# A hybrid encoder step on one core: 28 instead of 16 steps of the gates' projection ahead of the first attention scores, and two tiles instead of one for the near bias tables

## The chip, the core and the metric

The kernel runs on one core of a Trainium2 chip. A core has a matrix engine (TensorE, PE in the profile, its weight loads PEld), VectorE (DVE), ScalarE (ACT), GpSimd (POOL) and SyncE (SP). In this kernel SP and ACT issue nearly all DMA transfers. Each engine, and each issuing queue, works through its own list of instructions in order, and waits at an instruction until what that needs is there. The metric is the time of one execution in device microseconds (us), the median of several.

## The reference

One layer of an encoder over 2048 prompt rows and 32 sample rows, all in float32 (D_MODEL = 1024, 8 attention heads of 64 channels, chunks of 64 rows, each seeing itself and the 8 chunks before it). Cut to what matters here:

```python
h = rmsnorm(x, g_pre_mix) * (1 + scale_m) + shift_m
qa, ka, va, qb, kb, vb, gb, gk_low, gate_a, gate_b = split(h @ w_in)
bias = rel_bias[:, clip(i - j, -128, 128) + 128]                  # per head
ya = softmax(qa @ ka.T * 64 ** -0.5 + bias, over own + 8 chunks) @ va
yb = gated_linear_attention(qb, kb, vb, gk_low) ...
merged = sigmoid(gate_a) * (ya @ w_br_a) + sigmoid(gate_b) * (yb @ w_br_b)
x = x + gate_m * rmsnorm(merged @ w_out, g_post_mix)
x = x + gate_f * rmsnorm(conv_ffn(...), g_post_ffn)
```

## The kernel before

The activations `h` are kept on chip as a high and a low part (`hA`, `hB`, two arrays each); every product of matrices is three matmuls (`mm3`, L78 to L80): high x high, low x high, high x low. The program goes through five stages: the normalised input and a first projection, a projection with rows as outputs (`n_tile`, tiles `pn`), gated linear attention, band attention, and then merge, output projection and the gated MLP. PE's list is in the order in which the program is written; a scheduler orders the lists of the other engines and queues when the kernel is built.

**The near bias tables.** `bias_tables` (L454 to L473) is a generator, stepped once in every other `n_tile` through `side` beside `mod_late`, which streams rows of `w_ada` (tiles `wa2`, shown as `wa`) and adds them up on DVE (L484, L486). For each pair of heads `bias_tables` loads a tile `tr` from `rel_rev` (L464, issued by SP), turns it over with one matmul into `pb` (L467, two records each in the trace), writes `pb - cf` back into the same `tr` (L469, DVE), fills a corner (L471, DVE) and stores `tr` to `nbD` in DRAM (L472, issued by ACT). There is one buffer `tr`, so the load of a pair waits until the store of the pair before has landed.

**Attention and its filler.** `unit(h, g)` is one head's attention for 256 query rows (g = 8 is the sample); there are 72 units. A unit loads its queries (`q`, L977), every other unit a chunk of keys and values (L888, L892), and the first unit of a head the bias table `nb` (L908), all issued by SP. `scores` makes the scores of 128 query rows: matmuls into `PN` and `F` (L928, L929), bias and maximum on DVE (L936 to L944), the exponentials on ACT (L945, L948), the scaling of the tile `P` on POOL (L952). Each `P` is then transposed by PE (`pp`, L1019), split into two parts on ACT and DVE (`pth`, `ptl`) and multiplied with the values (`py`). Since the softmax of a unit takes a while, PE is given a filler between: `dense` with 16 chunks of 128 columns of the gates' projection (640 steps), then `branch_b` (160 steps). A step is one `mm3` of 128 x 416 outputs; eight steps make one output tile `pm`, which ACT passes through a tanh (L222) and stores to `sgT` (L230). A chunk is five tiles, so 40 steps; the weights of the next chunk are loaded (`wr`, L185) and split (L186 on ACT, L187 on DVE) while one runs.

The first unit has no unit before it, so its head is written out by hand (L1165 to L1172): the loads, 16 filler steps, the scores of its first 128 rows, 4 steps, its second scores, the loads of the next unit, 8 steps. What is left of the filler, `left`, is dealt out over the 72 units: a unit's quota follows from its own PE work, and within a unit its quota, its own transposes and products, the scores of the next unit (`S0_AT`, `S1_AT`) and the loads of the one after (`L_AT`) are sorted by due time.

Of the kernel before, what the change touches and what calls it, by code (L numbers as in the profile page):

```python
# [10 lines left out]
F32 = mybir.dt.float32  # L11
# [28 lines left out]
def dap(ap, offset, dims):  # L40
    return bass.AP(tensor=ap.tensor, offset=ap.offset + offset, ap=dims)
# [17 lines left out]
def encoder_step(ctx: ExitStack, tc: tile.TileContext, I, O):  # L59
    nc = tc.nc  # L60

    def pool(st, name, bufs=1, **kw):
        return st.enter_context(tc.tile_pool(name=name, bufs=bufs, reuse_waits="tile", **kw))
# [174 lines left out]
    with ExitStack() as st:  # L238
# [204 lines left out]
        wa = pool(late_st, "wada")  # L443
# [10 lines left out]
        def bias_tables():  # L454

            flip = wa.tile([128, 128], F32, name="flip")
            nc.gpsimd.memset(flip, 1.0)
            nc.gpsimd.affine_select(flip, flip, pattern=[[1, 128]], base=-127, channel_multiplier=1,
                                    compare_op=OP.is_equal, fill=0.0)
            cf = wa.tile([128, HA], F32, name="cf")  # L460
            nc.sync.dma_start(cf, dap(I["rel_rev"], 0, [[0, 128], [384, HA]]))
            for h in range(0, HA, 2):
                tr = wa.tile([128, 2, 256], F32, name="tr", tag="tr")
                nc.sync.dma_start(tr, dap(I["rel_rev"], h * 384, [[1, 128], [384, 2], [1, 256]]))  # L464
                yield
                p = psx.tile([128, 512], F32, name="pb", tag="px")
                nc.tensor.matmul(p, flip, tr.rearrange("p a b -> p (a b)"), start=True, stop=True)  # L467
                for j in range(2):
                    nc.vector.tensor_scalar(tr[:, j], p[:, 256 * j:256 * j + 256], cf[:, h + j:h + j + 1], None,  # L469
                                            op0=OP.subtract)  # L470
                nc.vector.memset(tr[0:64, :, 192:256], NEG)  # L471
                nc.scalar.dma_start(dap(nbD, h * 128 * 256, [[256, 128], [128 * 256, 2], [1, 256]]), tr)  # L472
                yield  # L473
# [76 lines left out]
        def side():  # L550

            yield from bias_tables()
            for blk in range(4, 12):
                yield from mod_late(blk)
            yield
            yield from mod_turn()
# [38 lines left out]
    def pull(stream, n):  # L595
        for _ in range(n):
            next(stream, None)
# [253 lines left out]
    with ExitStack() as st:  # L851
# [300 lines left out]
        def fill():  # L1152
            yield from dense(stg, [("g", i, 3088 + 128 * i) for i in range(16)], late_w.pop(1), ahead)
            yield from branch_b()

        filler = fill()
        units = [(h, g) for h in range(HA) for g in range(9)]
        left = 800 - 8
        us = [unit(*u) for u in units] + [None, None]

        def ustep(u):
            if u is not None:
                next(u)

        ustep(us[0])  # L1165
        pull(filler, 16)
        ustep(us[0])
        pull(filler, 4)
        ustep(us[0])
        ustep(us[1])  # L1170
        pull(filler, 8)
        left -= 28  # L1172

        own = [3 * {0: 3, 1: 6, 8: 3}.get(g, 9) for h, g in units]
        whole = (3 * left + sum(own)) / len(units)
# [1020 lines left out]
```

## Time and profile before

| | us |
|---|---|
| median of 3 executions | 3203.68 |
| lowest, highest | 3203.21, 3213.49 |
| the profiled execution, its own time | 3200.21 |
| span of its trace (first to last instruction) | 3198.5 |
| PE busy | 3075.2 |
| DVE busy | 2248.1 |
| ACT busy | 1654.4 |
| POOL busy | 550.0 |

The profile is one execution, taken by the hardware profiler. All instants below are us from the start of its span. PE's ends are modelled, so that a busy share of PE does not say that it runs at its peak. [...] A row of a timeline has the start, the duration, the engine, the line, the operation, what it writes and reads, and in brackets how long its engine was idle before it and what ended that.

### The profile page before, as it was taken

How to read it: one execution, taken by the hardware profiler on the slowest of the kernel's cores; microseconds unless marked ns; L12 is line 12 of the kernel's file. 1: busy time of each engine (PE TensorE's matmuls, PEld its weight loads, DVE VectorE, ACT ScalarE, POOL GpSimd, SP SyncE). 2: the span in 40 equal slices, each digit the busy share in tenths (PEclk: the TensorE clock that was granted, in tenths of full speed). 3: DMA queues.
4: the chain of work that ended last, by engine and by line, in shares of the span. 5: the costliest groups of instructions: out<-in, count | busy, mean ns of one | idle time of the engine just before them, and what ended most of it. 6: DMA issues, size and time to landing. Idle time of an engine off the chain costs nothing. (4 is left out here: it accounts for less than half of the span.)

```text
span 3198.5 us, 57346 instructions
## 1 busy us (share of the span) xinstructions
PE 3075.2 (96%) x19748; PEld 2963.9 (93%) x19748; DVE 2248.1 (70%) x4913; ACT 1654.4 (52%) x3856; POOL 550.0 (17%) x663
## 2 busy tenths in 40 slices
PE   6999999999999999999999899999999999999997
PEld 4899999998999999988999899999999999999997
DVE  6735517774555445566676799899888778998877
ACT  4412224443555545544444555567656556676755
POOL 2201201111111111111344433400000001310001
PEclk9999999999999999999999999999999999999998
DMA  7344435545333333576466676777987667888785
GB/s 224 104 137 129 141 104 137 140 127 139 110 114 102 101 97 114 163 230 197 131 191 190 207 246 208 227 240 223 263 246 217 192 189 207 273 248 287 236 276 148
DMA packets 601367, 580.21 MB, mean 181 GB/s; under 512 B 55761, under 2 KB 529570, under 8 KB 601074
## 3 DMA queue, kind: packets, MB, share of 16 engines
q1 hardware_dynamic: 556386, 528.93, 55.7%
q10 hardware_dynamic: 44432, 47.34, 4.6%
q8 instruction: 155, 2.54, 0.3%
q14 instruction: 138, 1.13, 0.1%
q0 software_dynamic: 256, 0.26, 0.0%
HBM read 388.71 MB, written 187.65 MB: 180 GB/s over the span
## 5 line engine op out<-in xcount | busy, mean ns | idle before, releaser
L78 PE MATMUL pm<-hA,wh 128*128 128x416 f32 x768 | 290.3, 378 | 0.0
L1740 PE MATMUL ad<-hA,hB 128*128 128x350 f32 (+2 forms) x1566 | 271.3, 324 | 6.7 <-ACT work L1866 3.4
L79 PE MATMUL pm<-hA,wh 128*128 128x416 f32 x768 | 270.2, 352 | 0.0
L80 PE MATMUL pm<-hA,wl 128*128 128x416 f32 x768 | 270.0, 352 | 0.0
L1682 DVE TENSOR_TENSOR hA<-raws,hA 128x512 fp32r<-128x512 f32 (+1 forms) x368 | 257.5, 708 | 16.5 <-ACT hA L1677 15.9
L1740 PEld LDWEIGHTS ad<-hA,hB 128*128 128x128 f32 x1566 | 255.2, 190 | 7.8 <-ACT work L1866 4.3
L1677 ACT ACTIVATE hA<-raws 128x512 fp32r<-128x512 f32 (+1 forms) x368 | 223.6, 617 | 36.0 <-DVE raws L1658 13.6
L1740 PE MATMUL ad<-hA,hA 128*128 128x348 f32 (+2 forms) x1362 | 235.0, 325 | 5.5 <-ACT g L1849 4.8
L1658 POOL TENSOR_TENSOR raws<-raws 128x512 f32<-128x512 f32 (+1 forms) x90 | 144.6, 1619 | 538.9 <-DMA raws<-in_w_down_dram 316.5
L1740 PE MATMUL g<-hA,hB 128*128 128x350 f32 (+2 forms) x1350 | 233.8, 323 | 3.0 <-ACT work L1862 1.6
L1740 PEld LDWEIGHTS ad<-hA,hA 128*128 128x128 f32 x1362 | 222.3, 190 | 7.0 <-ACT g L1849 5.1
L1740 PEld LDWEIGHTS g<-hA,hB 128*128 128x128 f32 x1350 | 218.8, 188 | 5.1 <-ACT work L1862 2.8
L1740 PE MATMUL ad<-hA 128*128 128x350 f32 (+2 forms) x1263 | 218.3, 323 | 4.4 <-ACT work L1866 4.3
L1740 PEld LDWEIGHTS ad<-hA 128*128 128x128 f32 x1263 | 204.5, 188 | 6.2 <-ACT work L1866 6.1
L1682 DVE TENSOR_TENSOR hB<-raws,hB 128x512 fp32r<-128x512 f32 (+1 forms) x287 | 203.5, 716 | 4.0 <-ACT hB L1677 3.9
L952 POOL TENSOR_SCALAR P<-P,mx 128x640 f32<-128x640 f32 (+5 forms) x136 | 103.3, 759 | 534.9 <-DVE mx L951 289.5
L1677 ACT ACTIVATE hB<-raws 128x512 fp32r<-128x512 f32 (+1 forms) x287 | 174.7, 616 | 27.3 <-DMA raws<-in_w_up_dram 11.0
L78 PE MATMUL pn<-wh,hA 128*128 128x256 f32 (+1 forms) x624 | 177.6, 285 | 0.0
L79 PE MATMUL pn<-wl,hA 128*128 128x256 f32 (+1 forms) x624 | 176.6, 283 | 0.0
L80 PE MATMUL pn<-wh,hA 128*128 128x256 f32 (+1 forms) x624 | 176.4, 283 | 0.0
L69 ACT ACTIVATE pth<-pp 128x256 fp32r<-128x256 f32 (+1 forms) x288 | 106.0, 373 | 133.6 <-PE pp L1019 123.1
L1849 ACT COPY g<-ad 128x348 f32<-128x348 f32 (+2 forms) x102 | 44.4, 435 | 230.7 <-PE ad L1740 154.2
(484 smaller groups left out, 8769.3 us busy)
## 6 DMA issues: line engine op xcount, KB each, us to landing
raws<-in_w_up_dram SPq DMA_DIRECT2D x220, 256.0 KB, 4.1
raws<-sW SPq DMA_DIRECT2D x176, 256.0 KB, 3.8
sW<-raws SPq DMA_DIRECT2D x88, 256.0 KB, 4.2
raws<-in_w_down_dram SPq DMA_DIRECT2D x80, 256.0 KB, 4.9
wr<-in_w_in_dram SPq DMA_DIRECT2D x76, 256.0 KB, 3.2
sgT<-tx ACTq DMA_DIRECT2D x80, 208.0 KB, 2.6
wa<-in_w_ada_dram SPq DMA_DIRECT2D x64, 256.0 KB, 2.9
keys<-ks SPq DMA_DIRECT2D x128, 128.0 KB, 3.0
```

The source lines that it names most:

```text
L69: i = nc.scalar.activation(hi, src, AF.Copy)
L78: nc.tensor.matmul(out, ah, bh, start=first and i == 0, stop=False)
L79: nc.tensor.matmul(out, ah, bl, start=False, stop=False)
L80: nc.tensor.matmul(out, al, bh, start=False, stop=last and i == n - 1)
L952: nc.gpsimd.tensor_scalar(P[:m, :tot], P[:m, :tot], mx[:m, 6:7], 1.0, op0=OP.mult, op1=OP.mult)
L1658: getattr(eng, op)(raw(out, n), raw(a, n), raw(b, n))
L1677: act = nc.scalar.activation(hi[:, :n], raw(i, n), AF.Copy)
L1682: nc.vector.tensor_sub(lo[:, :n], raw(i, n), f32(hi[:, :n]))
L1740: nc.tensor.matmul(out[:, :w], l_[:, k], r_[:, k, :w], start=first and k == 0 and i == 0, stop=k == n - 1 and i == 2, skip_group_check=True)
L1849: nc.scalar.copy(g[:, 0, :w], ad[:, 0, :w])
```

## The change

The diff, whole:

```diff
@@ -460,7 +460,7 @@
             for h in range(0, HA, 2):
-                tr = wa.tile([128, 2, 256], F32, name="tr", tag="tr")
+                tr = wa.tile([128, 2, 256], F32, name="tr", tag="tr", bufs=2)
                 nc.sync.dma_start(tr, dap(I["rel_rev"], h * 384, [[1, 128], [384, 2], [1, 256]]))
@@ -1163,13 +1163,13 @@
         ustep(us[0])
-        pull(filler, 16)
+        pull(filler, 28)
         ustep(us[0])
         pull(filler, 4)
         ustep(us[0])
         ustep(us[1])
         pull(filler, 8)
-        left -= 28
+        left -= 40
```

`tr` gets a second buffer, so that the load of a pair of heads waits for the store two pairs before. In the head of attention 28 steps of the filler stand between the loads of the first unit and its first scores. No operation is added or taken away. The 12 steps come out of the units' quotas: the units with g = 2 and g = 6 of each head (16 units) have 8 steps instead of 9, and the units (1,0), (3,0), (5,0) and (7,0) 15 instead of 14; the other 52 keep their number.

On SP's queue, at the first loads of the bias tables (`cf`, `tr`, then the stream of `wa` and the weights `wr` of the next projection), the difference is:

```order
 L461 DMA cf<-in_rel_rev_dram 128x8x1
-L464 DMA tr<-in_rel_rev_dram 128x2x256
+L464 DMA tr<-in_rel_rev_dram 128x2x256 x2
 L481 DMA wa_2000<-in_w_ada_dram 128x512
 L481 DMA wa_2004<-in_w_ada_dram 128x512
 L481 DMA wa_2059<-in_w_ada_dram 128x512
+L185 DMA wr<-in_w_in_dram 128x2x256 x2
 L481 DMA wa_2063<-in_w_ada_dram 128x512
```

The second table is loaded right behind the first; the third and the fourth load stand where the second and the third stood (behind `wa_2402` and `wa_2662`), and the place of the fourth is empty. Two weight loads go ahead of a `wa`.

On ACT, at the head of attention (`tx` is the tanh of a filler tile and `sgT` its store, `vs` the split of values, `P` the exponentials, `pth` the split of a transposed `P`, `wh` the split of the next chunk's weights), before:

```order
L222 ACTIVATE tx<-pm 128x416
L230 DMA sgT<-tx 128x416
L900 ACTIVATE vs<-vr 128x4x64
L945 ACTIVATE P,mx<-P,mx 128x128
L945 ACTIVATE P,mx<-P,mx 128x256
L900 ACTIVATE vs<-vr 128x4x64
L222 ACTIVATE tx<-pm 128x416
L230 DMA sgT<-tx 128x416
L69 ACTIVATE pth<-pp 128x256
```

and in the changed kernel, from the same place on:

```order
L222 ACTIVATE tx<-pm 128x416
L230 DMA sgT<-tx 128x416
L945 ACTIVATE P,mx<-P,mx 128x128
L900 ACTIVATE vs<-vr 128x4x64
L222 ACTIVATE tx<-pm 128x416
L230 DMA sgT<-tx 128x416
L945 ACTIVATE P,mx<-P,mx 128x256
L900 ACTIVATE vs<-vr 128x4x64
L186 ACTIVATE wh<-wr 128x512
L222 ACTIVATE tx<-pm 128x416
L186 ACTIVATE wh<-wr 128x512
L69 ACTIVATE pth<-pp 128x256
```

Here a `tx` with its store stands ahead of each of the first two exponentials, and the split of the weights of the chunk after next (`wh`, twice) stands ahead of the first `pth` instead of behind the exponentials of the next unit.

On SP, at the head of attention, before:

```order
L892 DMA vr<-vn 128x4x128
L977 DMA q_8757<-qs 128x256
L977 DMA q_8859<-qs 128x256
L977 DMA q_8965<-qs 128x256
L888 DMA keys_8746<-ks 64x512 x2
L888 DMA keys_8747<-ks 64x512 x2
L892 DMA vr<-vn 128x4x128
L977 DMA q_9099<-qs 128x256
L888 DMA keys_8746<-ks 64x512 x2
L888 DMA keys_8747<-ks 64x512 x2
```

and in the changed kernel:

```order
L977 DMA q_8757<-qs 128x256
L977 DMA q_8902<-qs 128x256
L977 DMA q_9019<-qs 128x256
L888 DMA keys_8746<-ks 64x512 x2
L888 DMA keys_8747<-ks 64x512 x2
L892 DMA vr<-vn 128x4x128
L888 DMA keys_8746<-ks 64x512 x2
L888 DMA keys_8747<-ks 64x512 x2
L977 DMA q_9139<-qs 128x256
```

Up to the queries of the first unit (`q_8757`) the queue is the same; the fourth query tile goes behind the third set of keys instead of ahead of it.

## Rows read from the trace of the kernel before

**Rows 1.** The page: busy time of the engines; the granted clock in 40 slices.
```profile
PE 3075.2 (96%) x19748; PEld 2963.9 (93%) x19748; DVE 2248.1 (70%) x4913; ACT 1654.4 (52%) x3856; POOL 550.0 (17%) x663
...
PEclk9999999999999999999999999999999999999998
```
**Rows 2.** Timeline of PE, 171 to 200: start, us, engine, what it did.
```profile
179.12 1.10 PE L467 MATMUL pb<-tr,flip 128*128 128x512 f32 x2 [1.65 <-DMA tr<-in_rel_rev_dram]
...
194.49 2.04 PE L467 MATMUL pb<-tr,flip 128*128 128x512 f32 x2 [2.92 <-DMA tr<-in_rel_rev_dram]
```
**Rows 3.** Timeline of SP's queue, then of ACT's, 120 to 230.
```profile
141.20 0.37 SPq L464 DMA_DIRECT2D tr<-in_rel_rev_dram  x1
...
174.83 0.37 SPq L464 DMA_DIRECT2D tr<-in_rel_rev_dram  x1
...
190.04 0.38 SPq L464 DMA_DIRECT2D tr<-in_rel_rev_dram  x1
...
170.87 0.39 ACTq L472 DMA_DIRECT2D nbD<-tr  x1
...
186.35 0.38 ACTq L472 DMA_DIRECT2D nbD<-tr  x1
```
**Rows 4.** Windows: length, busy us by engine, PE's granted clock, DMA share, GB/s.
```profile
191.50:194.40 2.90, 0.07 (x1) 0.00 (x0) 0.00 (x0) 0.37 (x1) 0.00 (x0) 1.00 0.86 231
194.40:197.80 3.40, 3.31 (x9) 2.31 (x10) 1.04 (x3) 0.00 (x0) 0.00 (x0) 0.50 0.07 23
```
**Rows 5.** Timeline of PE, 776 to 783.
```profile
777.24 0.35 PE L79 MATMUL pm<-hA,wh 128*128 128x416 f32 x1
777.43 0.35 PE L80 MATMUL pm<-hA,wl 128*128 128x416 f32 x1
782.69 0.47 PE L928 MATMUL PN<-keys,q 128*128 128x128 f32 x1 [4.91 <-DMA q<-qs]
```
**Rows 6.** Windows at the first scores.
```profile
777.78:782.69 4.91, 0.00 (x1) 0.00 (x1) 0.00 (x0) 0.82 (x2) 0.00 (x0) 0.88 0.90 278
782.69:788.32 5.63, 5.63 (x18) 5.41 (x19) 0.82 (x5) 0.61 (x3) 1.09 (x2) 0.50 0.37 101
```
**Rows 7.** Timeline of SP's queue, 700 to 800.
```profile
777.86 1.45 SPq L977 DMA_DIRECT2D q<-qs  x3
```
**Rows 8.** Timeline of ACT, 768 to 830.
```profile
767.98 0.63 ACT L186 ACTIVATE wh<-wr 128x512 fp32r<-128x512 f32 x1 [2.69 <-PE pm L79]
...
772.17 0.63 ACT L186 ACTIVATE wh<-wr 128x512 fp32r<-128x512 f32 x1 [0.75 <-ACT kr L215]
```
**Rows 9.** Waits of PE in attention, 790 to 1510, the longest in total.
```profile
PE F L929 <- DVE keys L72: 2.2, 8, 0.4
...
PE pp L1019 <- POOL P L952: 2.1, 4, 0.6
```
**Rows 10.** Timelines of POOL, 805 to 860, and PE, 821.9 to 831.2.
```profile
821.06 0.80 POOL L952 TENSOR_SCALAR P<-P,mx 128x640 f32<-128x640 f32 x1 [1.13 <-DVE mx L951]
...
829.06 0.80 POOL L952 TENSOR_SCALAR P<-P,mx 128x640 f32<-128x640 f32 x1 [0.78 <-DVE mx L951]
...
821.97 0.38 PE L1019 MATMUL pp<-ident,P 128*128 128x128 f32 x2
...
830.75 0.38 PE L1019 MATMUL pp<-ident,P 128*128 128x128 f32 x2
```
**Rows 11.** Waits of ACT in attention, 790 to 1350: total, times, longest.
```profile
ACT wh L186 <- PE pm L79: 8.2, 5, 2.5
```
**Rows 12.** Windows at two other idle gaps of PE, in the MLP and the merge.
```profile
2903.00:2906.00 3.00, 0.40 (x3) 0.17 (x2) 1.33 (x3) 2.60 (x5) 0.00 (x0) 1.00 1.08 371
2905.80:2912.00 6.20, 6.17 (x39) 6.17 (x40) 6.20 (x12) 2.81 (x6) 0.00 (x0) 1.00 1.02 348
1508.00:1512.00 4.00, 2.23 (x16) 1.82 (x15) 4.00 (x12) 2.19 (x7) 1.36 (x2) 0.99 0.55 179
1512.00:1515.30 3.30, 3.30 (x17) 3.30 (x16) 1.63 (x3) 0.84 (x2) 1.11 (x2) 0.50 0.51 145
```

## The prediction

> **What bounds the kernel now.** Read the page first: PE is busy for 3075.2 us of a span of 3198.5, 96 per cent, at nearly the full clock in every slice; DVE has 70 per cent, no other engine more [rows 1]. So the time is PE's own work plus the places where PE stands still or runs at the lower clock, and a change that adds no work and takes none away can only move those. The next views are therefore PE's timeline, read for the brackets, and the windows around each bracket, read for the granted clock. Both edits aim at one such place each.
>
> The first place is in the projection with rows as outputs. PE stands 1.65 us at the second `pb` and 2.92 us at the third, both times for the load of `tr` [rows 2]. SP's queue says why the loads are late: they go out at 174.83 and 190.04, 4.0 and 3.7 us behind the store of the pair before them (170.87 and 186.35) [rows 3]; with one buffer a load can't go before that store has landed. Behind the second gap the clock is granted at 0.50 from 194.4 to 197.8, after 1.00 in the window before [rows 4].
>
> The second place is the head of attention. PE has done its 16 filler steps and stands 4.91 us for the first queries [rows 5]. Behind that gap it runs 5.63 us at a granted 0.50 [rows 6]. Everywhere else in attention PE hardly waits: the largest entries from 790 to 1510 come to about 2 us each [rows 9].
>
> **The second `tr` buffer.** It removes the wait of the second load for the first store. That load now stands right behind the first, which left at 141.20 [rows 3], long before the second `pb`; the 1.65 us go. The third load takes the place of the second in SP's queue, and there it waits for the first store, as the second load did: it leaves near 174.8 and lands, with the 4.3 us that lie between 174.83 and 179.12, near 179, when it is wanted near 190. The 2.92 us go too. The fourth takes the place of the third and waits for the second store, leaves near 189 to 190, lands near 194, and is wanted near 202: between two `pb` lie four tiles of PE work, 11 us (180.2, the end of the second, to 191.5, where the wait for the third begins) [rows 2, 4]. So no load is late any more, and PE's timeline has no other bracket in this stretch that could come up next. With the second gap goes the half clock behind it: 3.31 us of busy PE at 0.50 are 1.65 us of lost work. Sum: 1.65 + 2.92 + 1.65 = 6.2 us.
>
> What it moves costs nothing: one more 0.37 us issue on SP ahead of the `wa` stream at 141, and two of the weights `wr` a place earlier. They belong to the next projection, behind the last `pb`, and PE waits for neither `wa` nor `wr` in this stretch.
>
> **The 12 steps ahead of the first scores.** A step is three matmuls 0.19 us apart [rows 5], so 12 steps are 36 x 0.19 = 6.8 us. PE, free at 777.6, would be done with them at 784.5. The queries were there at 782.69, and their place in SP's queue is the same, behind the first keys and values; they are issued at 777.86 [rows 7]. So the load is covered with 1.8 us to spare, and the 4.91 us go. With the gap goes the half clock behind it: 5.63 us at 0.50 are 2.8 us of lost work. Sum: 4.91 + 2.8 = 7.7 us.
>
> What hides what moves here? The filler's first chunk now ends just before the loop, at step 40, near 793, so the next chunk's weights are needed earlier than they were; ACT splits them at 767.98 and 772.17 [rows 8], some 20 us ahead: nothing. One more tanh stands ahead of the first exponentials on ACT, but its tile is finished at step 24, before the scores are. The fourth query tile goes behind the third set of keys on SP; it waits for a buffer that the second scores free, and with it out of the way the keys leave earlier: nobody loses.
>
> **Where the 12 steps are taken from.** Sixteen units lose one step of 0.56 us, four gain one. A step in a unit is cover for the softmax of the next: POOL's scaling must be done when the next unit's first transpose is due. In the usual unit it is done 0.9 us before (829.06 + 0.80 against 830.75); where a tanh of the filler falls into the chain, 0.1 us before (821.06 + 0.80 against 821.97) [rows 10]. The cost of a lost step thus lies between nothing (a gain is excluded, as the units lose cover and gain none) and the step itself where the chain is bound already, 16 x 0.56 = 9.0 us. I take 1.5 us: of the two rows the 0.9 us is the usual one, a unit with a step less loses only part of 0.56 us of cover, and only about one unit in four has the tanh in its chain; three or four of sixteen then pay close to a whole step, less what the four longer units give.
>
> **Sum.** 6.2 + 7.7 - 1.5 = 12.4 us. Against the profiled execution, 3200.21, that is 3187.8. The median of the three executions is 3.5 us above it, so the forecast for the median is 3203.7 - 12.4 = **3191.3 us**.
>
> **The clock elsewhere.** Everything behind 195 runs 6 to 14 us earlier. Does the clock behave the same at the other gaps? In the rows it doesn't follow from the length of a gap alone: at 2903 PE stands 2.60 us of a 3 us window and goes on at 1.00, and at 1509 it stands for under 2 us and the next 3.3 us are granted at 0.50 [rows 12]. A drop there costs 3.30 x 0.5 = 1.65 us. I take no net change, and two drops either way, 3.3 us, for the range. [...]
>
> **Rivals.**
> - *The softmax becomes the bound in the short units.* Then all sixteen pay a whole step, and 13.9 - 9.0 = 4.9 us remain: 3198.8. For it: cover of 0.1 us in some units [rows 10]. Against it: PE's waits for POOL's `P` come to 2.1 us in four places over 64 such units [rows 9].
> - *The gap at the first scores stays*, because the queries land later than 784.5, behind a queue that is busier than before (the DMA engines are at 0.90 there [rows 6]). Then only the tables' part is left: 6.2 - 1.5 = 4.7 us, 3199.0. Against it: the queue ahead of them is unchanged, and 1.8 us are to spare.
> - *The gain is taken back later*, by a stage that is paced by its transfers: the DMA share is over 1.0 in the MLP at 2903 to 2912 [rows 12]. If the loads there ran at a pace of their own, PE would only wait more: 3203.7, no change. Against it: PE is busy for 6.17 of 6.20 us in that very window, so it sets the pace.
> - *Slower: the weight splits hold ACT.* In the changed order the two splits of the chunk after next stand ahead of the first `pth` on ACT. Such a split can't start before the last matmul of the chunk whose weights it writes over, and all of ACT's softmax work queues behind it. Before, ACT waited so in five places, 8.2 us, the longest 2.5 [rows 11]. If the new order brings a hold of 2.5 us at each of the 15 changes of chunk, with 0.9 us of cover, PE loses 1.6 us each, 24 us, less the 13.9 gained: some 10 us slower, 3213.8. It decides from the point where a hold is longer than 0.9 us in most places. Against it: at the first change the split's condition (step 40, near 793) comes before the transposes for which `pth` waits in any case.
>
> **How the numbers follow.** Forecast (10 to 16 us gained): 0.70. Short units bound, or the gap at the first scores stays: 0.10 and 0.06. Taken back later: 0.07. Slower: 0.07. The range goes down to the forecast with no cost in the units and two drops fewer, 3203.7 - 13.9 - 3.3 = 3186.5, a little below for the modelled ends of PE, which make gaps look shorter, 3185.5; and up to 3199.5, which takes in the first two rivals. About 0.3 per cent (9.6 us, so 3194.1) is what a measurement of this kernel can tell from no change. Faster than that: 0.71, nearly all of the forecast and a little of the first rival; the same: 0.22; slower: 0.07.
>
> **What would show it.** In the new profile the brackets for `tr` at the second and third `pb`, and for `q` at the first `PN`, should be gone or below 0.5 us, and the granted clock 1.00 in both places; the third `pb` should start near 190, the first `PN` near 778 (784.5 less the 6.2 of the tables). The waits of PE in attention should grow by one to two us at `pp` for `P`. The prediction is wrong if a bracket at `q` is left (the load was not late by the queue but by what ran beside it), if the waits at `pp` or `F` in attention grow by over 4 us (the cover was thinner than read), or if the three brackets are gone and the span is not shorter (a later stage holds the pace).

## The result and the profile after

| | us |
|---|---|
| before, median of 20 executions (lowest, highest) | 3211.1 (3200.69, 3215.84) |
| after, median of 20 executions (lowest, highest) | 3214.99 (3207.55, 3224.7) |
| ratio after to before, with its 95 per cent interval | 1.0017 [1.0009, 1.0025] |
| the profiled execution of after, its own time | 3214.13 |

The changed kernel is slower, by 0.17 per cent of 3211.1, about 5.5 us. 12.4 us of gain had been forecast. The executions of one kernel spread over some 15 us, and the profiled execution of before, 3200.21, is faster than all 20 in the table. So the two traces are compared place by place, and sizes are taken from many executions.

PE runs the same number of matmuls in both, so the n-th can be set beside the n-th. The trace of after is 13.9 us longer than that of before: 3.8 us are lost ahead of the bias tables, 6.6 gained there and 7.0 at the first scores; 4.1 are lost between 868 and 1300 and 12.5 between 1300 and 1400 (on the clock of before); and 6.7 behind 1400; the rest is small. The first and the last of these are hardly the change's: against the same trace of before, the kernel with the 28 steps alone (below) is 1.9 us late at the second `pb`, its wait left out (179.41 against 177.47), and the one with the second buffer alone loses 7.1 us behind 1396.

The page says as little as in [rows 1]: the same work, and PE as busy as before.

```profile
span 3212.4 us, 57351 instructions
...
PE 3082.0 (96%) x19748; PEld 2967.2 (92%) x19748; DVE 2251.3 (70%) x4913; ACT 1653.7 (51%) x3856; POOL 546.4 (17%) x663
```

**Both gaps are gone, as forecast.** PE's timeline at the bias tables, the answer to [rows 2]: the second and the third `pb` have no bracket.

```profile
181.16 1.02 PE L467 MATMUL pb<-tr,flip 128*128 128x512 f32 x2
...
193.37 1.02 PE L467 MATMUL pb<-tr,flip 128*128 128x512 f32 x2
```

In [rows 2] the second `pb` would have started at 177.47 without its gap; here everything ahead of the tables is 3.7 us later already. So 193.37 is 189.7 on the clock of before, near the 190 of the prediction. At the first scores the first `PN` has no bracket either, the answer to [rows 5]; 781.17 less the same 3.7 is 777.5, where the prediction had 778:

```profile
781.17 0.22 PE L928 MATMUL PN<-keys,q 128*128 128x128 f32 x1
```

The windows in both places (length, busy us of PE, PEld, DVE, ACT and POOL, PE's granted clock as a share of full speed, DMA share, GB/s) answer [rows 4, 6]: PE busy all the time, clock 1.00, no stretch at 0.50.

```profile
185.00:200.00 15.00, 15.00 (x124) 14.52 (x123) 9.89 (x18) 1.49 (x4) 0.00 (x0) 1.00 0.67 204
776.00:782.00 6.00, 6.00 (x35) 5.95 (x34) 0.32 (x3) 0.94 (x2) 0.73 (x1) 1.00 0.92 283
782.00:788.00 6.00, 6.00 (x34) 5.96 (x33) 1.05 (x6) 1.92 (x6) 1.59 (x3) 1.00 0.83 227
```

**The loss is in attention, in two places above all.** The larger one lies between 1310 and 1400, at the end of the gates' projection and the start of `branch_b`. PE's waits there (total, times, longest), first of before, where six entries come to 3.6 us:

```profile
PE PN L928 <- DVE mx L936: 0.9, 2, 0.5
...
```

and of after, where seven come to 11.7:

```profile
PE py L1038 <- DVE ptl L72: 3.0, 4, 1.5
PE py L1038 <- ACT pth L69: 2.1, 1, 2.1
PE PN L928 <- DVE mx L936: 2.1, 1, 2.1
PE F L929 <- DVE keys L72: 1.8, 1, 1.8
PE pm L78 <- ACT hA L69: 1.3, 1, 1.3
...
```

So 8.1 us more. The windows of after show two stretches at half clock besides, behind the first and the last of the longer gaps; in before the whole stretch from 1310 to 1400 is granted 1.00.

```profile
1329.30:1332.75 3.45, 3.45 (x14) 3.13 (x13) 0.84 (x2) 1.18 (x3) 0.00 (x0) 0.51 0.79 225
1387.40:1390.80 3.40, 3.08 (x14) 2.77 (x15) 1.44 (x7) 1.33 (x5) 0.00 (x0) 0.50 0.79 243
```

In the first of them a step of the filler takes 1.15 us (from 1329.89 to 1331.04, clock 0.50), ahead of it 0.56 (from 1328.35 to 1328.91, clock 1.00), so about half of PE's busy time at half clock is lost. Half of 3.45 and of 3.08 us of busy PE is 3.3 us, so this stretch costs 8.1 + 3.3 = 11.4 us. One more gap that before does not have, 1.47 us at `py` for `ptl`, follows in head 7 (1429.17).

**What holds PE there** is read from three timelines of after. PE first:

```profile
1326.28 0.38 PE L1038 MATMUL py<-pth,vs 128*128 128x256 f32 x1 [2.10 <-ACT pth L69]
1328.13 0.38 PE L1038 MATMUL py<-ptl,vs 128*128 128x256 f32 x1 [1.47 <-DVE ptl L72]
```

ACT, which makes `pth`:

```profile
1323.25 1.67 ACT L69 ACTIVATE hB<-ybr 128x832 fp32r<-128x832 f32 x2
1324.82 1.14 ACT L69 ACTIVATE hB<-wbr 128x512 fp32r<-128x512 f32 x2
1325.86 0.53 ACT L69 ACTIVATE pth<-pp 128x256 fp32r<-128x256 f32 x2
```

DVE, which makes `ptl`:

```profile
1324.17 2.37 DVE L72 TENSOR_TENSOR hB<-ybr,hB 128x832 fp32r<-128x832 f32 x2 [0.42 <-ACT hB L69]
1326.46 1.28 DVE L72 TENSOR_TENSOR hB<-wbr,hB 128x512 fp32r<-128x512 f32 x2
1327.66 0.61 DVE L72 TENSOR_TENSOR ptl<-pp,pth 128x256 fp32r<-128x256 f32 x2
```

Two `pth` start only behind 2.7 us of other splits on ACT, and two `ptl` behind 3.5 us on DVE. Those splits make the first operand (`ybr`) and weights (`wbr`) of `branch_b`, the work that follows the gates' projection in the filler. They are issued by the filler itself: `ahead(3)`, called near the projection's end, writes them out, with ACT's half kept in program order (`keep=True`). In before the same burst stands behind the last two `pth` of its unit; ACT's timeline there:

```profile
1325.40 0.37 ACT L69 ACTIVATE pth<-pp 128x256 fp32r<-128x256 f32 x1
...
1327.37 0.27 ACT L69 ACTIVATE pth<-pp 128x128 fp32r<-128x128 f32 x1
1327.88 1.69 ACT L69 ACTIVATE hB<-ybr 128x832 fp32r<-128x832 f32 x2 [0.24 <-ACT pth L69]
1329.47 1.14 ACT L69 ACTIVATE hB<-wbr 128x512 fp32r<-128x512 f32 x2
```

The orders of the two programs on ACT had this before any run, before:

```order
L945 ACTIVATE P,mx<-P,mx 128x256
L948 ACTIVATE P,mx<-F,mx 128x384
L69 ACTIVATE pth<-pp 128x256
L945 ACTIVATE P,mx<-P,mx 128x256
L948 ACTIVATE P,mx<-F,mx 128x384
L222 ACTIVATE tx<-pm 128x416
L69 ACTIVATE pth<-pp 128x128
L230 DMA sgT<-tx 128x416
L69 ACTIVATE hB_676<-ybr 128x832 x2
L69 ACTIVATE hB_677<-wbr 128x512 x2
```

and after:

```order
L945 ACTIVATE P,mx<-P,mx 128x256
L948 ACTIVATE P,mx<-F,mx 128x384
L945 ACTIVATE P,mx<-P,mx 128x256
L948 ACTIVATE P,mx<-F,mx 128x384
L69 ACTIVATE hB_676<-ybr 128x832 x2
L69 ACTIVATE hB_677<-wbr 128x512 x2
L69 ACTIVATE pth<-pp 128x256
L69 ACTIVATE pth<-pp 128x128
```

Both `pth` went from ahead of the burst to behind it. The reason is a count: with 12 steps more ahead of the loop and one step less in 12 of the units up to head 5, three of them made good in (1,0), (3,0) and (5,0), the filler is 12 - 12 + 3 = 3 steps further when unit (6,0) begins. The burst is tied to a step of the filler (624), the `pth` to the unit, so the two slid past each other. The later gaps are of the same kind. The `mx` for which `PN` waits 2.05 us (1367.91) stands on DVE right behind a split of `wbr`, and the split of the sample's keys for which `F` waits 1.76 us (1387.72) right behind one of `wr` (1386.37, on DVE); the 1.28 us at `pm` (1359.91) are a step of `branch_b`, come too early for its operand.

```profile
1366.82 0.69 DVE L72 TENSOR_TENSOR hB<-wbr,hA 128x512 fp32r<-128x512 f32 x1 [2.15 <-ACT hA L69]
1367.43 0.42 DVE L936 CUSTOM_DVE_ANT_0 P<-PN,nb 128x256 f32<-128x256 f32 x1
```

**The smaller place is the short units, the eight with g = 6.** In a unit with 8 steps one step, no longer two, stands between the last transposes (`pp`) and the `py` of their split. PE's timeline at unit (1,6) of after (one L80 is one step):

```profile
936.34 0.38 PE L1019 MATMUL pp<-ident,P 128*128 128x128 f32 x2
...
937.17 0.35 PE L80 MATMUL pm<-hA,wl 128*128 128x416 f32 x1
937.36 0.28 PE L1038 MATMUL py<-pth,vs 128*128 128x256 f32 x1
937.96 0.39 PE L1038 MATMUL py<-ptl,vs 128*128 128x256 f32 x1 [0.33 <-DVE ptl L72]
```

and at the same unit of before, with two:

```profile
941.16 0.38 PE L1019 MATMUL pp<-ident,P 128*128 128x128 f32 x2
...
942.01 0.35 PE L80 MATMUL pm<-hB,wl 128*128 128x416 f32 x1
942.57 0.35 PE L80 MATMUL pm<-hB,wl 128*128 128x416 f32 x1
942.76 0.28 PE L1038 MATMUL py<-pth,vs 128*128 128x256 f32 x1
942.88 0.28 PE L1038 MATMUL py<-ptl,vs 128*128 128x256 f32 x1
```

The two `py` start 0.60 us apart instead of 0.12. With the two places that follow, the unit loses 1.3 us; in the units (0,6) and (2,6) to (5,6) the starts of `py` are late by 0.4 to 0.7 us, and in the units with g = 2, just as short, by nothing. In (1,6) the splits of the next chunk's weights stand in front of `ptl` on DVE (after):

```profile
936.29 1.16 DVE L187 TENSOR_TENSOR wl<-wr,wh 128x512 fp32r<-128x512 f32 x1
937.38 0.20 DVE L942 TENSOR_SCALAR mx<-mx 128x1 f32<-128x1 f32 x1
937.50 0.41 DVE L72 TENSOR_TENSOR ptl<-pp,pth 128x256 fp32r<-128x256 f32 x1
```

In (0,6) and (2,6) to (5,6) it is the order on DVE that sets g = 6 apart. The maximum (`mx`, L942) of the next unit's second scores stands behind a `ptl` there; with g = 2, and with g = 6 in before, it stands ahead of it. DVE, then ACT, in (3,2) of after, where the last pair of `pp` starts at 1073.95:

```profile
1073.67 0.21 DVE L942 TENSOR_SCALAR mx<-mx 128x1 f32<-128x1 f32 x1
...
1073.87 0.42 DVE L72 TENSOR_TENSOR ptl<-pp,pth 128x256 fp32r<-128x256 f32 x1
...
1075.04 0.37 ACT L69 ACTIVATE pth<-pp 128x256 fp32r<-128x256 f32 x1
```

and in (3,6), where it starts at 1109.57:

```profile
1109.49 0.42 DVE L72 TENSOR_TENSOR ptl<-pp,pth 128x256 fp32r<-128x256 f32 x1
1109.82 0.21 DVE L942 TENSOR_SCALAR mx<-mx 128x1 f32<-128x1 f32 x1
...
1111.19 0.37 ACT L69 ACTIVATE pth<-pp 128x256 fp32r<-128x256 f32 x1
1111.58 0.52 ACT L222 ACTIVATE tx<-pm 128x416 f32<-128x416 f32 x1
```

In those five units `mx` starts 0.1 to 0.3 us behind that pair, in the g = 2 units up to head 5 about 0.3 us ahead of it. The exponentials wait for `mx`, the last `pth` stands behind them on ACT, and it starts 1.4 to 1.7 us behind the `pp` instead of 1.0 to 1.1. It isn't a tanh of the filler: in (3,6) that stands behind the last `pth`, and in (0,2) and (4,2) one stands ahead of the last exponentials and nothing is lost. This cause is read from the trace: no run moved `mx` alone, and what put `ptl` ahead of it when DVE's list was made was not tried.

Over 432 us of attention (868 to 1300, ending in head 5) PE gets through 2625 matmuls in after where it got through 2649 in before; 24 of 432/2649 us each are 3.9 us, near the sum of the losses in the five short units with g = 6 in it.

```profile
868.00:1300.00 432.00, 425.90 (x2625) 395.01 (x2623) 216.67 (x830) 214.35 (x646) 77.45 (x106) 1.00 0.37 108
```

### The profile page after: what moved, and what is told of

It reads as the page before. It is cut to its first block, busy times and chain, and to the rows that moved or that the text cites. A ratio compares the mean times of both kernels' runs of the same rounds, so it can differ in the third digit from the quotient of the medians.

```text
span 3212.4 us, 57351 instructions
## 1 busy us (share of the span) xinstructions
PE 3082.0 (96%) x19748; PEld 2967.2 (92%) x19748; DVE 2251.3 (70%) x4913; ACT 1653.7 (51%) x3856; POOL 546.4 (17%) x663
## 5 line engine op out<-in xcount | busy, mean ns | idle before, releaser
L80 PE MATMUL pm<-hA,wl 128*128 128x416 f32 x768 | 269.8, 351 | 0.0
L80 PE MATMUL pn<-wh,hA 128*128 128x256 f32 (+1 forms) x624 | 176.2, 282 | 0.0
```

Of the source, the lines that this page charges most:

```text
L80: nc.tensor.matmul(out, al, bh, start=False, stop=last and i == n - 1)
```

## The experiments

Each kernel was measured beside the kernel before. The ratio with its interval is the one on record; it is not the quotient of the two medians beside it, and the two differ by up to 0.0014. Gains and losses in us below go by the ratio.

The theory: the two edits give what was forecast, and the gain is lost to (a) the place of `branch_b`'s splits, three steps early against the units, and (b) the short units. The rivals: (b) alone, or a loss that needs neither (the tables, or what the 28 steps move in the queues).

**The second buffer alone.** The kernel before with

```diff
-                tr = wa.tile([128, 2, 256], F32, name="tr", tag="tr")
+                tr = wa.tile([128, 2, 256], F32, name="tr", tag="tr", bufs=2)
```

> The kernel before with the second buffer for the bias tables alone. If both gains are real and the loss comes from the attention's filler, the two waits for the table go and the run is 6.2 us faster than before (ratio 0.998). If gains ahead of attention are taken back by a later stage, the waits go and the time is that of before (1.000).

Measured: 3205.73 against 3208.51, ratio 0.9986 [0.9978, 0.9995], so about 4.5 us faster (1.6 to 7.1). The trace of after has this stretch 6.6 us shorter; the forecast of 6.2 lies inside the interval.

**The 28 steps alone.** The kernel before with `pull(filler, 28)` and `left -= 40`.

> The kernel before with the 28 steps alone: one `tr` buffer, so both gaps of the bias tables stay; the quotas, and the order on ACT and DVE from the start of attention on, are those of the changed kernel. If the two edits add up, it should stand where the changed kernel does plus what the second buffer saves: the changed kernel measured +5.5 us (1.0017), the second buffer alone -4.5 us (0.9986), so +8 to +12 us against the kernel before, a ratio of 1.0025 to 1.0037, with the gap at the first scores gone and the gaps of about 2 us at `py` behind branch B's operand splits (near 1330) there. The rival, that the loss needs both edits at once (some phase between the tables and attention), would give a ratio of 1.000 or below, since the 7.7 us at the first scores are won in any case.

Measured: 3221.45 against 3211.9, ratio 1.0027 [1.0016, 1.0038], 8.7 us slower. With the 4.5 us of the buffer that gives +4.2 us for both; after measured +5.5. Within these intervals the edits add up, and all of the loss is the second one's. PE's waits between 1310 and 1400 are nearly those of after, with 3.2 and 2.1 us at `py`.

**The phase alone.** The kernel before, one buffer and 16 steps, with three steps moved into unit (5,8), so that everything from (6,0) on stands as in after:

```diff
             quota = min(left, round(due)) if x < len(units) - 1 else left
             due -= quota
             left -= quota
+            if (h, g) == (5, 8):
+                quota += 3
+            elif (h, g) in ((7, 0), ):
+                quota += 1
+            elif h > 5 and g in (2, 6):
+                quota -= 1
```

> The kernel before (16 steps, one table tile) with three filler steps more in unit (5,8) and the changed kernel's quotas from unit (6,0) on, so that branch B of the filler starts at the same step of the same unit, (6,3), as in the changed kernel; nothing else is changed. Theory of the phase: the 10 to 12 us lost at 1305 to 1400 come from where branch B's operand splits fall on ACT and DVE, so this run shows the idle gaps at the products py near 1328 and is 10 to 13 us slower than before (1.003 to 1.004). Rival, cover: the loss comes from the 12 steps that attention as a whole has less; here it has as many as before, so the time is that of before (1.000).

Measured: 3220.84 against 3208.51, ratio 1.0035 [1.0023, 1.0046], 11.2 us slower, with neither of the change's edits in it. Two of its units are short ones with g = 6; the rest is put down to the phase. PE's timeline has the pair of gaps:

```profile
1329.14 0.38 PE L1038 MATMUL py<-pth,vs 128*128 128x256 f32 x1 [2.10 <-ACT pth L69]
1330.99 0.58 PE L1038 MATMUL py<-ptl,vs 128*128 128x256 f32 x1 [1.46 <-DVE ptl L72]
```

**Both edits, with the twelve steps taken so that the phase stays.** After, with `left -= 28` again, so that the units' quotas are those of before, and the twelve steps taken by hand in heads 0 to 5; first from the units g = 2 and g = 6, which are then as short as in after:

```diff
-        left -= 40
+        left -= 28
 ...
             quota = min(left, round(due)) if x < len(units) - 1 else left
             due -= quota
             left -= quota
+            if h < 6 and g in (2, 6):
+                quota -= 1
```

> The changed kernel, but the 12 steps are all taken from the units g = 2 and g = 6 of heads 0 to 5, so that from (6,0) on each unit has the steps and the start of the kernel before. Theory of the phase: the loss at 1305 to 1400 is gone, each short unit pays about 0.4 us at a product py, and the run is about 9 us faster than before (0.997). Rival, cover: the 12 steps are missing as in the changed kernel, so it is 5 us slower than before (1.0017).

Measured: 3204.98 against 3208.51, ratio 0.9986 [0.9976, 0.9996], 4.5 us faster, half of what was expected, so the short units seem to cost more than 0.4 us each. All six with g = 6 have `ptl` ahead of `mx` on DVE, or a weights' split, as in after. Then from g = 0 and g = 8, which have the most steps (`g in (0, 8)` in the same line), so that no unit has 8:

> As the last, but the 12 steps are taken from the units g = 0 and g = 8 of heads 0 to 5, which have 14 or 15 steps. Theory of the phase: these units have cover to spare (3.6 us of it at g = 8 in the trace of before), so nothing is paid and the run is 13 to 14 us faster than before (0.9957). Rival, cover: no better than the run with short units.

Measured: 3197.02 against 3208.51, ratio 0.9964 [0.9951, 0.9977], 11.5 us faster, and faster than both kernels. The gaps of 2.10 and 1.47 us at `py` are gone; PE's waits between 1310 and 1400 (its page has the same work):

```profile
PE F L928 <- ACT keys L69: 2.4, 1, 2.4
...
PE py L1038 <- ACT pth L69: 0.7, 1, 0.7
```

What follows: the two edits are worth nearly what was forecast if the steps are taken from units that can spare them. The two intervals overlap by a hair, so the price of the twelve short units, 0.0022 (give or take 0.0016) or 7 us, is a rough one. It is not the price of their length alone either, since the two kernels also differ in the steps that come at each unit of heads 0 to 5.

**How far the phase may slide.** The last kernel with 2 steps less, or 2 or 3 more, in (5,8), given back in (7,8):

```diff
+            if (h, g) == (5, 8):
+                quota += 3
+            elif (h, g) == (7, 8):
+                quota -= 3
```

> As the run with 12 steps from the wide units (g = 0 and 8 of heads 0 to 5), but branch B starts two steps later in unit (6,3) (each unit from (6,0) on starts at a filler step lower by 2). The burst of splits for branch B's first operand stays behind the last two pth of unit (6,1) on ACT. If the place of the burst decides, no idle gap at the products near 1315 to 1330 and a time like the wide run's, 0.996 to 0.998 of before; if any shift of the filler costs, 1.000 or more.

> As the wide run, with branch B two steps earlier, as in the changed kernel at (6,3), and no unit of heads 6 and 7 shortened but the last. The burst now stands ahead of one pth on ACT (of two in the changed kernel). If the place of the burst decides, one gap of about 1.5 us at a product py, further ones behind it, and 5 to 10 us more than the wide run: 0.998 to 1.000 of before. If the short units of heads 6 and 7 made the loss, it is as fast as the wide run, 0.9964.

> As the last with three steps, so that the burst stands ahead of two pth on ACT exactly as in the changed kernel. If the place of the burst decides, the gaps of 2.1 and 1.5 us at py come back and the run is 8 to 12 us slower than the wide run, 0.999 to 1.000 of before; if the short units of heads 6 and 7 made the loss, 0.9964.

| shift in steps | ratio to before |
|---|---|
| -2 | 0.9962 [0.9949, 0.9975] |
| 0 | 0.9964 [0.9951, 0.9977] |
| +2 | 0.9984 [0.9973, 0.9996] |
| +3 | 0.9992 [0.9982, 1.0003] |

Two steps, with the burst ahead of one `pth`, cost 0.0020 (give or take 0.0017), and the longest wait of PE at `py` between 1310 and 1400 is 1.2 us there. Three steps cost 0.0028 (give or take 0.0017), 9 us, with no unit of 8 steps up to head 5, and the gaps are back in PE's timeline of the +3 kernel:

```profile
1321.59 0.39 PE L1038 MATMUL py<-pth,vs 128*128 128x256 f32 x1 [2.23 <-ACT pth L69]
1323.58 0.58 PE L1038 MATMUL py<-ptl,vs 128*128 128x256 f32 x1 [1.61 <-DVE ptl L72]
```

With -2 one gap of 4.13 us appears at `pp` for POOL's `P` (1352.98), and behind it, from there to some 1357.6, a step takes 1.19 us instead of 0.56, as at half clock; so each place of the burst has gaps of its own. Whether this one costs anything in the end is not settled: by the ratios nothing (-0.0002, give or take 0.0018, which leaves room for 5 us), by the medians, 3204.49 against 3212.21, some 4 us. The +3 kernel has the burst where after, at 1.0017, has it, and its steps taken from g = 0 and g = 8 instead of g = 2 and g = 6: 0.0025 (give or take 0.0013), 8 us over eight heads, 1 us each. The timeline has 0.4 to 1.3 in each unit with g = 6 up to head 5.

**The first burst one tile later.** After, with the splits of `ahead` at the last chunk's tile `i` = 4, eight filler steps later:

```diff
-            elif i == 3:
+            elif i == 4:
```

> The changed kernel with the splits of branch B's first operand and weights written one tile (8 filler steps) later, at the fifth tile of the last chunk instead of the fourth; nothing else is moved. On ACT the burst then stands behind the last two pth of unit (6,1) and ahead of two pth of the next. If the burst makes the gaps at 1324 to 1328, they go from there (3.6 us and a stretch of half clock, 1.7 us), and unless the next pth are hit as hard the run is 3 to 5 us faster than the changed kernel, 0.9985 to 1.0005 of before. If the gaps come from something else, they stay.

Measured: 3214.48 against 3212.21, ratio 0.9998 [0.9986, 1.001]. How much of the loss comes back is not settled: by the ratio it is 0.0019 (give or take 0.0014) better than after, 6 us; by its medians it is still 2.3 us slower than before; and in its trace the stretch from 1300 to 1400 is only 1.2 us shorter than in after. The pair at `py` is gone, and in its place PE's timeline has

```profile
1332.41 0.41 PE L1019 MATMUL pp<-ident,P 128*128 128x128 f32 x2 [2.42 <-DVE mx L942]
```

since the burst now stands ahead of the next unit's maximum on DVE (the splits of `ybr` and `wbr` run from 1328.77 to 1331.93, the `mx` of L942 starts at 1332.17). The later gaps (2.2 at `PN`, 1.8 at `F`, 1.3 at `pm`) stay. So the first burst decides the first pair of gaps, and moving it alone trades that pair for another gap.

## Why the prediction was wrong

- **The second `tr` buffer** was right: both brackets and the half clock went, third `pb` at the forecast time, 6.6 us in the trace against 6.2; alone it measured 4.5 [1.6, 7.1].
- **The 12 steps ahead of the first scores** were right in mechanism: no bracket at `q`, clock 1.00. In the trace of after the place gains 7.0 us against before, of 7.7 forecast. Against other executions that would differ: the bracket at `q` was 4.91 us in before and 5.51 in the kernel with the second buffer alone, which keeps the 16 steps. Both edits with the steps taken elsewhere give 11.5 us of the 13.9 forecast for the two.
- **Where the 12 steps are taken from** is the step that failed, twice. First, it priced a lost step at POOL's `P` [rows 10], the cover of the next unit. Those waits did not grow: 2.1 us before [rows 9], 2.3 after. The step was missing inside the unit, between the last `pp` and its `py`, where nothing had been looked at. That only some units pay was right, but not which and why: it is those with g = 6, eight units of sixteen instead of three or four. In the trace what delays them up to head 5 is the order on DVE or a weights' split, not a tanh, and (1,6) pays 1.3 us, more than the step. The term of 1.5 us measured 7 to 8, in two rough differences, close to the upper bound of 9.0. Of the rivals, "the softmax becomes the bound in the short units" had this size, by another wait.
- Second, it counted how many steps a unit has, and not at which unit a given step now comes. The filler is not uniform: some of its steps issue splits on ACT and DVE, and a shift of three steps put 2.7 and 3.5 us of them ahead of `pth` and `ptl`. No term of the sum had this; it measured 9 us. The trace of before could not show it, but the two orders on ACT, shown above, could, had they been read at that place as they were at the head of attention.
- **The slower rival** had the kind of cause right, splits that stand ahead of `pth`, and the place wrong. It named a hold of ACT by the weights' splits (`wh`) at each change of chunk; those holds did not grow, 8.2 us in [rows 11], and the weights cost PE 1.3 us in one unit, (1,6). In after

```profile
ACT wh L186 <- PE pm L79: 5.8, 5, 2.9
```

- **The sum** in the terms that were measured, with the phase's 9 and the units' 8 us, is -13.9 + 9 + 8 = +3 us, against +5.5 [2.9, 8.0]. The forecast also stood on a low base: the median of three executions, 3203.68, is 7.4 us below that of 20. A gain of 12.4 us would have given 3198.7, still within the range, so it is not the base that made the prediction wrong. The two drops of the clock either way in that range were the author's estimate from one place [rows 12]; no run measured their number, and the mean granted clock was 0.988 in the trace of before and 0.987 in that of after.
- **Still open**: which of the later gaps (1.28 at `pm`, 2.05 at `PN`, 1.76 at `F`) carries how much of the 9 us; only the first burst was moved by itself. What the gap of 4.13 us costs with the shift by -2. And why DVE's list has `ptl` ahead of `mx` in the short units with g = 6 and not in those with g = 2.

## What to carry to other kernels

Filler that is dealt out in steps is not only time on PE: some steps issue work on the engines on which the main chain depends, and a shift of two or three steps can put that work ahead of what PE needs next (it cost 0.0020 and 0.0028 of the time here, each give or take 0.0017). So when steps are moved, count at which unit each such step comes, in the order of every engine, not only how long each unit is. And take filler from the units that have the most of it: the last step between a transpose and the product of its split cost 0.4 to 1.3 us here, for a step of 0.56.

## What the runs showed that was not expected

The load of the sample's cached keys (`ck`) came with very different delays, in one kernel where nothing around it was changed. PE's timeline of that one, with the second buffer alone:

```profile
1379.41 0.37 PE L928 MATMUL F<-keys,q 128*32 128x384 f32 x1 [3.50 <-ACT keys L69]
```

In the profiles of before and after this wait is 0.70 and 0.69 us, in the others up to 4.30, and behind the 4.30 (the kernel with the steps taken from g = 2 and g = 6 of heads 0 to 5) there is a stretch at half clock:

```profile
1380.80:1386.40 5.60, 5.40 (x21) 4.55 (x22) 3.92 (x12) 2.86 (x9) 0.48 (x1) 0.50 0.66 195
```

That is 3.6 + 2.7 = 6.3 us in one place, which may be part of the spread of some 15 us between executions of one kernel (one profile of each kernel can't tell). What delays the load was not tried.
